# Attention's values products as split products over pairs of heads, and a state update over all 128 rows, in a two-layer hybrid decoder

## The chip, the core and the metric

The kernel runs on one core of a Trainium2 chip. The metric is the device time of one execution in microseconds. Five engines work side by side, each through its own instructions in order: TensorE (PE; its weight loads are shown apart as PEld), VectorE (DVE), ScalarE (ACT), POOL and SP, which issues all transfers. TensorE writes into PSUM, here eight banks of 128x512 float32.

## The reference

Two layers of a decoder over 512 prompt tokens and 64 sample tokens (8 sequences of 8). In each layer one widened projection feeds two branches, retention and sparse attention; both are gated, projected and merged. The parts that the change touches are these, cut to their core:

```python
# sparse attention, per query block of 128 (q: 8 heads of 64, 2 key/value heads)
score = einsum('bths,bth->bts', relu(logits), iw * IDX_HEADS ** -0.5)
_, sel = top_k(where(causal, score, -inf), topk)
att = einsum('btkgd,btjkd->btkgj', qg, kg) * ATT_HEAD_DIM ** -0.5
p = softmax(where(valid, att, -inf))
o = einsum('btkgj,btjkd->btkgd', p, vg)          # the values product
u_a = einsum('bte,ed->btd', o * silu(az), w_o_att)
# retention, state of a sequence after its chunk (4 heads, 128x128 each)
S = S * decay_s + einsum('bchd,bche->bhde', kc * decay_k, vc)
```

All is float32; the kernel's result has to agree with it closely, so operands of fast products are split into a leading part and a remainder.

## The kernel before

Activations lie as 128 rows by tokens: `xh` and `xl` are the leading part and the remainder of the normalised input (float32r, a faster form of float32 on TensorE). Weights come in units of 128x1024, land in `wst` and are split into `whi` (ScalarE) and `wlo` (VectorE) by `convert`. A projection (`proj_a`) runs three products per block, `xh*whi`, `xl*whi` and `xh*wlo`, 288 columns each, into a `pm` bank. These are the "main" or "ordinary" products; 611 of them stand between 160 and 324 us.

Work is written as generators (streams): projections in the order of `PLAN`, and beside them streams for the indexer's top-k, for prompt attention (`attend`), for the samples' attention (`attend_s`) and for retention (`ret_p`, `ret_s`). `Streams.go` picks one instruction at a time: the one whose engine and inputs a model says are free first, ties by priority. It keeps a clock per engine, durations from `_duration`, and hops between engines from `HOP` plus a margin. The instruction is emitted there, so every row of the profile has this one line, L293. What the table says thus sets the order on each engine, and that order is then fixed; the engines meet on the chip only through semaphores.

Attention for query block j (0 to 3), head by head (`head`, three in flight): two score products into the bank `tq`, a softmax on VectorE and ScalarE in a tile of `t2k`, j+1 transposes into the bank `ta`, a ScalarE copy to another `t2k`, and j+1 values products into the bank `oT`. A values product has V as its weights (128 rows by 64 columns, in a part of a tile that the profile names `xl`), so it uses half of the array's columns, the tile form 128\*64; both operands are plain float32, and each such product is two records in the trace. A bank `oT` gathers all eight heads of a block, then one VectorE product of 128x512 gates it into `silz`.

The samples' state update (`ret_s`, per head and group g) multiplies the masked values `vt` (512 columns; leading parts on 64 rows, remainders on the other 64) by `kh`, the leading part of the keys on both halves, and then by `kl`, the keys' remainder, on 64 rows only, the tile form 64\*128. Both go into one `tr` bank. `kh`, `kl`, `vt` are tiles `iqs` in the profile.

POOL does the powers of the norms, 128x2 to 128x5, and nothing else of weight. At the end of a layer's attention, `layer` waits until all side streams are emitted, and then splits the gated branches `silz` into `oh` and `ol` for the output weights (the merge).

Of the kernel before, what the change touches and what calls it, by code (L numbers as in the profile page):

```python
# [105 lines left out]
class Op:  # L106
    __slots__ = ("eng", "fn", "a", "k", "name", "outs", "ins", "dur")

    def __init__(self, eng, fn, name, a, k):
# [4 lines left out]
        self.outs = [_box(x) for x in (out, acc) if x is not None]  # L114
        self.ins = [_box(x) for x in aps if x is not out and x is not acc]
# [26 lines left out]
def _duration(eng, name, out, aps, a, k):  # L142
    n = max(_free(x) for x in aps)
    psum = any(x.space == PSUM for x in aps[1:])
    if eng == "PE":
# [3 lines left out]
        if lhs.dtype == FT:  # L149
            if _free(lhs) <= 32:  # L150
                return 0.030 + n * 0.4e-3
            return 4 * max(n, 64) / 2.4e3 * (0.55 if _free(lhs) <= 64 else 1.0)
        return max(n, 64) / 2.4e3 + 0.003
# [10 lines left out]
    if eng == "POOL":  # L164
        return 0.3 + 0.165 * n
# [29 lines left out]
class Streams:  # L195
    """Emits the instructions of many sequential streams in the order in which a model of the engines could
    start them, so that each engine's program order follows what is ready."""
# [5 lines left out]
    def __init__(self):  # L203
# [5 lines left out]
        self.count = 0  # L209

# [66 lines left out]
    def go(self):  # L277
        clock = self.clock
        while True:
# [13 lines left out]
            op.fn(*op.a, **op.k)  # L293
            end = start + op.dur
# [10 lines left out]
def tile_hybrid_decoder(ctx: ExitStack, tc: tile.TileContext, A, O):  # L305
# [30 lines left out]
    def r3(ap, a):  # L336
        return ap.rearrange("p (a b) -> p a b", a=a)
# [54 lines left out]
    # ---- weights: one ordered sequence of units, each split into two float32r parts as it lands  # L392
# [164 lines left out]
    def layer(l, xh, xl, kxb):  # L557
# [32 lines left out]
        av = r3(raw[1][:, ro + 1152:ro + 1792], 5)  # L590
# [20 lines left out]
        T2 = slots(at, "t2k", [128, 512], FT, NSLOT["t2"])  # L611
# [66 lines left out]
        def kx(j, ps):  # L678
# [6 lines left out]
            kk = r3(kkt[:n], 3)  # L685
            yield S.activation(kkt[:n], src[:, 0:192], AF.Copy, scale=r)
            yield S.activation(av[:n, j], src[:, 192:320], AF.Copy, scale=r)
# [30 lines left out]
            yield SP.dma_start(O["v"][l, rows], av[:n, j])  # L718
# [179 lines left out]
        def head(j, u, g, kv, oT, done):  # L898
            L = max(256, (j + 1) * 128)
            bias = con("cb") if j == 0 else scs[j]  # L900
            q = qst[j, u][:, (g % 2) * 2 + kv]
            P = yield Get(T2)
# [5 lines left out]
            PT = yield Get(T2)  # L908
            pT = yield Get(BANK["ta"])
            W_ = (j + 1) * 128  # L910
            for k in range(j + 1):
                yield PE.transpose(pT[:, k * 128:(k + 1) * 128], P[:, k * 128:(k + 1) * 128], ident)
            K.put(T2, P)
            yield S.activation(PT[:, :W_], pT[:, :W_], AF.Copy)
            K.put(BANK["ta"], pT)
            for k in range(j + 1):
# [634 lines left out]
```

## Time and profile before

| | us |
|---|---|
| timed runs (3) | 1131.04, 1131.97, 1132.43; median 1131.97 |
| span of the profiled execution | 1130.3 |
| TensorE busy, matmul / weight loads | 1116.5 / 1058.9 |
| VectorE busy | 725.6 |
| ScalarE busy | 512.5 |
| POOL busy | 45.7 |

The profiled execution is told by its span, from the first to the last instruction; of its time outside the span the profile says nothing, so the span is set beside the median of the timed runs, 1.7 us longer. Busy times are unions of records, which may overlap: a matmul's record holds its way through the array, so a stream of products looks busy throughout, and the starts of its records tell how fast it runs. The granted clock of TensorE is 1.00 in every stretch (2.4 GHz).

### The profile page before, as it was taken

Reading aid. Unit: us, or ns where it says so; the run is one execution under the profiler, and the core shown is the slowest. Engines: PE = TensorE matmul, PEld = TensorE weight load, DVE = VectorE, ACT = ScalarE, POOL = GpSimd, SP = SyncE. Lnnn points to the kernel's source line nnn. Section 1 sums busy time; section 2 is a strip of 40 time slices with the busy share of each in tenths; the row PEclk is TensorE's granted clock in tenths of the full one; section 3 lists DMA queues with packets and bytes.
Section 4 is the critical chain, followed back from the end, with each engine's and each line's share of the span. In section 5 each row is a group of like instructions: output and inputs, shape, how many; then the busy total and the mean of one; then the engine's idle time right before and its main releaser. Section 6 shows DMA issues by size and latency. Waiting matters only on the chain.

```text
span 1130.3 us, 21562 instructions
## 1 busy us (share of the span) xinstructions
PE 1116.5 (99%) x8586; PEld 1058.9 (94%) x8586; DVE 725.6 (64%) x1883; ACT 512.5 (45%) x1084; POOL 45.7 (4%) x52
## 2 busy tenths in 40 slices
PE   8999999999999999999999999999999999999998
PEld 7899988888899999999999999888889999999998
DVE  6799988876464444543658999888654553544343
ACT  6643566647443232324546336656563422222331
POOL 0100200000000000000010012000000000000000
PEclk9999999999999999999999999999999999999999
DMA  6442221322122222523336112222212222234231
GB/s 196 139 133 76 76 75 52 102 78 78 59 75 75 93 76 92 172 92 109 100 118 181 59 57 94 74 79 80 73 60 78 75 78 91 75 130 144 93 113 48
DMA packets 43895, 105.92 MB, mean 94 GB/s; under 512 B 6418, under 2 KB 18578, under 8 KB 43794
## 3 DMA queue, kind: packets, MB, share of 16 engines
q1 hardware_dynamic: 43794, 104.55, 27.4%
q8 instruction: 67, 1.10, 0.4%
q14 instruction: 34, 0.28, 0.1%
HBM read 93.61 MB, written 10.91 MB: 92 GB/s over the span
## 4 chain that ended last, share of the span: by engine, by line
PE 91%; DVE 4%; DMA 2%; ACT 2%; issue 1%; SPq 0%; POOL 0%; DVEq 0%; ACTq 0%; POOLq 0%
PE pm L293 72%; PE oT L293 5%; PE tq L293 4%; PE acc L293 3%; PE tr L293 3%; PE ta L293 3%; DVE wlo L293 1%; DMA wst<-in_wb 1%; ACT whi L293 1%; DVE misc L293 1%; DMA x<-in_xT 1%; DVE silz L293 0%; DMA wst<-in_wq 0%; DVE qs L293 0%; DVE ol L293 0%
## 5 line engine op out<-in xcount | busy, mean ns | idle before, releaser
L293 PE MATMUL pm<-xl,whi 128*128 128x288 f32 x1536 | 458.7, 299 | 0.0
L293 PE MATMUL pm<-xh,wlo 128*128 128x288 f32 x1536 | 458.4, 298 | 0.0
L293 PE MATMUL pm<-xh,whi 128*128 128x288 f32 x1536 | 458.0, 298 | 0.4 <-DVE misc L293 0.4
L293 PEld LDWEIGHTS pm<-xl,whi 128*128 128x128 f32 x1536 | 290.1, 189 | 3.2 <-issue 2.4
L293 PEld LDWEIGHTS pm<-xh,whi 128*128 128x128 f32 x1536 | 290.2, 189 | 2.9 <-issue 1.6
L293 PEld LDWEIGHTS pm<-xh,wlo 128*128 128x128 f32 x1536 | 289.9, 189 | 1.8 <-issue 1.4
L293 ACT ACTIVATE whi<-wst 128x1024 fp32r<-128x1024 f32 (+4 forms) x148 | 150.5, 1019 | 280.5 <-PE pm L293 207.7
L293 DVE TENSOR_TENSOR wlo<-wst,whi 128x1024 fp32r<-128x1024 f32 (+4 forms) x148 | 173.0, 1171 | 88.8 <-ACT whi L293 88.5
L293 PE MATMUL pm<-whi,xh 128*128 128x256 f32 (+2 forms) x416 | 117.2, 288 | 0.7 <-ACT xl L293 0.7
L293 PE MATMUL pm<-wlo,xh 128*128 128x256 f32 (+2 forms) x416 | 117.0, 289 | 0.0
L293 PE MATMUL pm<-whi,xl 128*128 128x256 f32 (+2 forms) x320 | 91.0, 284 | 0.0
L293 DVE TENSOR_TENSOR misc<-pm,R 128x288 f32<-128x288 f32 x64 | 29.2, 457 | 90.1 <-PE pm L293 88.7
L293 ACT ACTIVATE t2k<-t2k,sm 128x256 f32<-128x256 f32 (+3 forms) x136 | 75.6, 581 | 22.6 <-DVE sm L293 19.4
L293 PEld LDWEIGHTS pm<-whi,xh 128*128 128x128 f32 x416 | 78.7, 189 | 2.5 <-issue 1.2
L293 PEld LDWEIGHTS pm<-wlo,xh 128*128 128x128 f32 x416 | 78.7, 189 | 1.6 <-issue 1.1
L293 PE MATMUL pm<-oh,whi 128*128 128x288 f32 x240 | 71.0, 296 | 0.0
L293 PE MATMUL pm<-oh,wlo 128*128 128x288 f32 x240 | 70.9, 296 | 0.0
L293 PE MATMUL pm<-ol,whi 128*128 128x288 f32 x240 | 70.9, 295 | 0.0
L293 PEld LDWEIGHTS pm<-whi,xl 128*128 128x128 f32 x320 | 60.5, 189 | 0.1
L293 ACT ACTIVATE misc<-misc 128x288 f32<-128x288 f32 x64 | 27.9, 436 | 60.5 <-DVE misc L293 60.5
L293 DVE MAX8 sm<-xl 128x8 f32<-128x384 f32 (+2 forms) x96 | 52.3, 548 | 0.3
L293 DVE SCALAR_TENSOR_TENSOR misc<-misc,pm 128x288 f32<-128x288 f32 x60 | 26.8, 451 | 39.3 <-PE pm L293 39.3
(231 smaller groups left out, 1654.3 us busy)
## 6 DMA issues: line engine op xcount, KB each, us to landing
wst<-in_wa SPq DMA_DIRECT2D x96, 512.0 KB, 3.5
wst<-in_wb SPq DMA_DIRECT2D x16, 512.0 KB, 4.1
wst<-in_wo SPq DMA_DIRECT2D x16, 512.0 KB, 3.4
s<-in_ckv SPq DMA_DIRECT2D x32, 128.0 KB, 2.4
s<-in_s SPq DMA_DIRECT2D x8, 512.0 KB, 4.3
out_rss<-s SPq DMA_DIRECT2D x8, 512.0 KB, 2.6
x<-in_xT SPq DMA_DIRECT2D x8, 288.0 KB, 4.5
misc<-in_xT SPq DMA_DIRECT2D x8, 288.0 KB, 3.6
```

Source lines behind the costliest of these rows:

```text
L293: op.fn(*op.a, **op.k)
```

## The change

Values products go by pairs of heads (`pair`, two pairs in flight). V is split once per block of 128 tokens into `vhl`: for each key/value head 128 columns, 64 leading and 64 remainder. The two heads' softmaxes (`score`) run as streams of their own; their transposes go in chunks of up to two blocks into one `ta` bank, 256 or 512 columns. ScalarE copies the chunk to `pth` (float32r) and VectorE takes the remainder `ptl`; there is one tile of each. Each block then takes two products with `vhl` as weights, 128 rows by 128 columns, and 256 columns of `pth` or `ptl`. The `oT` bank holds two pairs, the two halves of its rows being the sums with V's leading part and with its remainder; `collect` adds the halves (a ScalarE copy and a VectorE addition per key/value head, 64x256) and POOL multiplies by the gate. The state's `kl` is written to all 128 rows, so its second product also runs over 128 rows. The table of durations gets new numbers for TensorE, a small price for a change of tile form, and a price per column for POOL's products that are no power.

```diff
--- before.py
+++ after.py
@@ -112,6 +112,7 @@
         out = k.get("out", a[0] if a else None)
         acc = k.get("accum_out")
         self.outs = [_box(x) for x in (out, acc) if x is not None]
+        self.form = (_val(a[1].partition_size) > 64, min(2, _free(a[1]) - 1 >> 5)) if eng == "PE" else None
...
@@ -149,8 +150,8 @@
         if lhs.dtype == FT:
             if _free(lhs) <= 32:
                 return 0.030 + n * 0.4e-3
-            return 4 * max(n, 64) / 2.4e3 * (0.55 if _free(lhs) <= 64 else 1.0)
-        return max(n, 64) / 2.4e3 + 0.003
+            return 2 * max(0.11, n / 1.2e3 + 0.005)
+        return max(0.108, (n + 32) / 2.4e3)
...
     if eng == "POOL":
-        return 0.3 + 0.165 * n
+        return 0.3 + (0.165 if k.get("op", a[-1]) == OP.pow else 0.0022) * n
...
@@ -291,6 +293,9 @@
             op = st[3]
             start = best[0][0]
             op.fn(*op.a, **op.k)
+            if op.form != self.form and op.eng == "PE":
+                start += 0.09
+                self.form = op.form
             end = start + op.dur
...
+            if j < 4:
+                for i, (h, o) in enumerate(((0, 64), (192, 128))):
+                    vh = vhl[:, j, h:h + 64]
+                    yield S.activation(vh, v[:, i * 64:(i + 1) * 64], AF.Copy)
+                    yield V.tensor_tensor(vhl[:, j, o:o + 64], v[:, i * 64:(i + 1) * 64], vh.bitcast(FT), OP.subtract)
             K.put(T2, kt2)
@@ -895,53 +910,87 @@
             yield S.activation(P, P, AF.Copy, scale=s)
             K.put(SM, sm)
 
-        def head(j, u, g, kv, oT, done):
+        def score(j, q, kv, P):
             L = max(256, (j + 1) * 128)
             bias = con("cb") if j == 0 else scs[j]
-            q = qst[j, u][:, (g % 2) * 2 + kv]
-            P = yield Get(T2)
             b = yield Get(BANK["tq"])
             ps = b[:, :L]
             yield PE.matmul(ps, q, kdh[:, 1 + kv, :L], start=True, stop=False)
             yield PE.matmul(ps, q, kdl[:, 1 + kv, :L], start=False, stop=True)
             yield from softmax(ps, bias, P[:, :L], b)
-            PT = yield Get(T2)
-            pT = yield Get(BANK["ta"])
-            W_ = (j + 1) * 128
-            for k in range(j + 1):
-                yield PE.transpose(pT[:, k * 128:(k + 1) * 128], P[:, k * 128:(k + 1) * 128], ident)
-            K.put(T2, P)
-            yield S.activation(PT[:, :W_], pT[:, :W_], AF.Copy)
-            K.put(BANK["ta"], pT)
-            for k in range(j + 1):
-                yield PE.matmul(oT[kv * 64:(kv + 1) * 64, g * 128:(g + 1) * 128], av[:, k, kv * 64:(kv + 1) * 64],
-                                PT[:, k * 128:(k + 1) * 128], start=k == 0, stop=k == j)
-            K.put(T2, PT)
-            K.put(HD, None)
+
+        def pair(j, u, kv, oT, first, done):
+            Ps, evs = [], []
+            for i in range(2):
+                P = yield Get(T2)
+                ev = Event()
+                K.spawn(then(score(j, qst[j, u][:, i * 2 + kv], kv, P), ev), PRIO["attend"])
+                Ps.append(P)
+                evs.append(ev)
+            o = oT[:, kv * 256:(kv + 1) * 256]
+            for k0 in range(0, j + 1, 2):
+                ks = range(k0, min(k0 + 2, j + 1))
+                w = len(ks) * 256
+                pT = yield Get(BANK["ta"])
+                for i in range(2):
+                    yield evs[i]
+                    for k in ks:
+                        yield PE.transpose(pT[:, (k - k0) * 256 + i * 128:(k - k0) * 256 + (i + 1) * 128],
+                                           Ps[i][:, k * 128:(k + 1) * 128], ident)
+                if ks[-1] == j:
+                    for P in Ps:
+                        K.put(T2, P)
+                    K.put(HD, None)
+                hi = yield Get(PTH)
+                lo = yield Get(PTL)
+                yield S.activation(hi[:, :w], pT[:, :w], AF.Copy)
+                yield V.tensor_tensor(lo[:, :w], pT[:, :w], hi[:, :w].bitcast(FT), OP.subtract)
+                K.put(BANK["ta"], pT)
+                for k in ks:
+                    for x in (hi, lo):
+                        yield PE.matmul(o, vhl[:, k, kv * 128:(kv + 1) * 128], x[:, (k - k0) * 256:(k - k0 + 1) * 256],
+                                        start=not first, stop=k == j and x is lo, skip_group_check=True)
+                        first.append(None)
+                K.put(PTH, hi)
+                K.put(PTL, lo)
             K.set(done)
 
-        HD = Slots([None] * HEADS_IN_FLIGHT)
+        HD = Slots([None] * PAIRS_IN_FLIGHT)
+
+        def collect(j, u, oT, done):
+            yield done
+            t = yield Get(T2)
+            o = t[:, :256]
+            for kv in range(2):
+                mine, other = slice(kv * 64, kv * 64 + 64), slice(64 - kv * 64, 128 - kv * 64)
+                c = slice(kv * 256, (kv + 1) * 256)
+                yield S.activation(o[mine], oT[other, c], AF.Copy)
+                yield V.tensor_tensor(o[mine], oT[mine, c], o[mine], OP.add)
+            K.put(BANK["oT"], oT)
+            yield e_az
+            z = silz[1][:, 2 * u:2 * u + 2, j * 128:(j + 1) * 128]
+            yield G.tensor_tensor(z, r3(o, 2), z, OP.mult)
+            K.put(T2, t)
...
         def attend():
             yield e_k
+            last = []
             for j in range(4):
                 if j:
                     yield e_sc[j]
-                oT = yield Get(BANK["oT"])
-                done = Event(8)
                 for u in range(2):
                     yield e_q[j, u]
-                    for g in (2 * u, 2 * u + 1):
-                        for kv in range(2):
-                            yield Get(HD)
-                            K.spawn(head(j, u, g, kv, oT, done), PRIO["attend"])
-                yield done
-                for u in range(2):
+                    oT = yield Get(BANK["oT"])
+                    done, first = Event(2), []
+                    for kv in range(2):
+                        yield Get(HD)
+                        K.spawn(pair(j, u, kv, oT, first, done), PRIO["attend"])
+                    last.append(Event())
+                    K.spawn(then(collect(j, u, oT, done), last[-1]), PRIO["attend"])
+                    yield done
                     K.put(QS, qst[j, u])
-                yield e_az
-                z = silz[1][:, :, j * 128:(j + 1) * 128]
-                yield V.tensor_tensor(z, r3(oT, 4), z, OP.mult)
-                K.put(BANK["oT"], oT)
+            for ev in last:
+                yield ev
...
@@ -1146,12 +1195,14 @@
             ins, vs = t["ins"], vr[:NS, 4, hc]
             g8 = math.exp(8 * lg[h])
             ks = yield Get(IQS)
-            kh, kl, vh = ks[:, 0], ks[:NS, 1], ks[:, 2]
+            kh, kl, vh = ks[:, 0], ks[:, 1], ks[:, 2]
             yield V.memset(ins[:NS, NS:96], 0.0)
             yield V.tensor_tensor(ins[:NS, :NS], b[:NS, :NS], con("blk", NS), OP.mult)
             yield S.activation(kh[:NS], b[:NS, 128:256], AF.Copy, scale=g8)
             yield S.activation(kh[NS:], b[:NS, 128:256], AF.Copy, scale=g8)
-            yield V.scalar_tensor_tensor(kl, b[:NS, 128:256], g8, kh[:NS].bitcast(FT), op0=OP.mult, op1=OP.subtract)
+            for rows in (slice(0, NS), slice(NS, 128)):
+                yield V.scalar_tensor_tensor(kl[rows], b[:NS, 128:256], g8, kh[:NS].bitcast(FT), op0=OP.mult,
+                                             op1=OP.subtract)
             K.put(BANK["tr"], b)
...
@@ -1182,7 +1233,7 @@
                                       bc(con("mk")[:, g * 4:g * 4 + 4, None], [128, 4, 128]), OP.mult)
                 pn = yield Get(BANK["tr"])
                 yield PE.matmul(pn, kh, flat(vt), start=True, stop=False)
-                yield PE.matmul(pn, kl, flat(vt)[:NS], start=False, stop=True)
+                yield PE.matmul(pn, kl, flat(vt), start=False, stop=True)
...
 PLAN = _plan("kx iq rv0 rv1 az0 az1 az2 az3 aq0 aq1 rt0 rt1 rt2 rt3")
-HEADS_IN_FLIGHT = 3
+PAIRS_IN_FLIGHT = 2
 PRIO = dict(convert=0, load=1, tables=6, indexer=7, indexer_s=3, attend=3, attend_s=5, ret_p=6, ret_s=4)
-NSLOT = dict(s4=3, qs=5, t2=5, hi=3, lo=3)
+NSLOT = dict(s4=3, qs=4, t2=5, pt=1, hi=3, lo=3)
```

How this moves instructions is shown at three places of layer 1, near the end of attention. TensorE, before: heads of block 3 (`oT` are values products, `ta` transposes, `tq` scores, `pm` main products).

```order
L293 MATMUL pm_68<-xh,wlo_93 128x288
L293 MATMUL pm_68<-xh,whi_90 128x288
L293 MATMUL oT_73<-t2k_386,xl 64x128 x4
L293 MATMUL ta_72<-cst,t2k_385 128x128 x4
L293 MATMUL tq_71<-kdh,qs_378 128x512
L293 MATMUL tq_71<-kdl,qs_378 128x512
L293 MATMUL pm_68<-xl,whi_90 128x288
```

And now, the last two pairs of block 3 but one chunk:

```order
L295 MATMUL oT_73<-pth_392,vhl 128x256
L295 MATMUL pm_68<-xh,whi_90 128x288
L295 MATMUL pm_68<-xl,whi_90 128x288
L295 MATMUL pm_68<-xh,wlo_93 128x288
L295 MATMUL pm_68<-xh,whi_90 128x288
L295 MATMUL pm_68<-xl,whi_90 128x288
L295 MATMUL oT_73<-ptl_393,vhl 128x256
L295 MATMUL oT_73<-pth_392,vhl 128x256
L295 MATMUL oT_73<-ptl_393,vhl 128x256
L295 MATMUL ta_72<-cst,t2k_395 128x128 x2
L295 MATMUL ta_72<-cst,t2k_397 128x128 x2
L295 MATMUL pm_68<-xh,wlo_93 128x288
```

Four products of a head in a row have become products in a chain of one, then three; the product of `ptl` stands behind five main products, and the next chunk's transposes follow it directly.

VectorE, before, at the gating of the last `oT` bank of layer 1 (`xh`, `iqs`: retention of the samples; `misc`: a gate's projection):

```order
L293 MEMSET xh 64x32
L293 TENSOR_TENSOR xh<-tr_74,cst 64x64
L293 SCALAR_TENSOR_TENSOR iqs_375<-tr_74,iqs_375 64x128
L293 TENSOR_TENSOR iqs_375<-xh,iqs_375 64x128
L293 TENSOR_TENSOR silz_358<-oT_73,silz_358 128x4x128
L293 TENSOR_TENSOR misc<-pm_69,R 128x288
```

And now, from the third last chunk's remainder to the last additions:

```order
L295 TENSOR_TENSOR ptl_393<-ta_72,pth_392 128x512
L295 TENSOR_TENSOR gs_406<-gs_406,cst 128x4
L295 SCALAR_TENSOR_TENSOR gs_406<-gs_406 128x4
L295 TENSOR_TENSOR misc<-pm_69,R 128x288
L295 TENSOR_TENSOR wlo_92<-wst_87,whi_89 128x1024
L295 TENSOR_TENSOR ptl_393<-ta_72,pth_392 128x512
L295 TENSOR_TENSOR silz_367<-tr_74,silz_367 128x512
L295 TENSOR_TENSOR misc<-pm_70,R 128x288
L295 TENSOR_TENSOR ptl_393<-ta_72,pth_392 128x512 x2
L295 TENSOR_TENSOR misc<-pm_68,R 128x288
L295 TENSOR_TENSOR wlo_93<-wst_88,whi_90 128x1024
L295 TENSOR_TENSOR t2k_396<-oT_73,t2k_396 64x256 x2
```

The one product on `oT` is gone; remainders `ptl` stand between weight conversions `wlo` and evacuations, and two additions on `oT` follow.

POOL, before, the last powers of layer 1's retention:

```order
L293 TENSOR_TENSOR gs_394<-rsm_96,mh 128x2
L293 TENSOR_TENSOR gs_395<-rsm_97,mh 128x4
L293 TENSOR_TENSOR gs_394<-rsm_98,mh 128x2
L293 TENSOR_TENSOR gs_395<-rsm_96,mh 128x4
L293 TENSOR_TENSOR gs_394<-rsm_97,mh 128x2
L293 TENSOR_TENSOR gs_395<-rsm_98,mh 128x4
```

And now, to the end of layer 1:

```order
L295 TENSOR_TENSOR silz_368<-t2k_396,silz_368 128x2x128
L295 TENSOR_TENSOR gs_405<-rsm_97,mh 128x2
L295 TENSOR_TENSOR silz_368<-t2k_396,silz_368 128x2x128
L295 TENSOR_TENSOR gs_406<-rsm_98,mh 128x4
L295 TENSOR_TENSOR silz_368<-t2k_396,silz_368 128x2x128
```

The gating products `silz` stand between the powers, in one queue; the last stands behind the last power.

## Rows read from the trace of the kernel before

**Rows 1.** The page: busy us by engine, and the chain of waits by engine
```profile
PE 1116.5 (99%) x8586; PEld 1058.9 (94%) x8586; DVE 725.6 (64%) x1883; ACT 512.5 (45%) x1084; POOL 45.7 (4%) x52
...
PE 91%; DVE 4%; DMA 2%; ACT 2%; issue 1%; SPq 0%; POOL 0%; DVEq 0%; ACTq 0%; POOLq 0%
```

**Rows 2.** Busy us (instructions) by stretch: PE, PEld, DVE, ACT, POOL; clock; DMA
```profile
0.00:57.00 57.00, 49.79 (x358) 47.81 (x359) 39.83 (x125) 37.77 (x86) 5.46 (x10) 1.00 0.53 168
57.00:113.00 56.00, 56.00 (x435) 53.44 (x435) 53.10 (x155) 21.37 (x44) 2.38 (x2) 1.00 0.31 103
160.00:324.00 164.00, 163.65 (x1323) 143.16 (x1323) 114.19 (x358) 93.90 (x231) 6.81 (x8) 1.00 0.21 73
334.00:580.00 246.00, 246.00 (x1848) 245.99 (x1847) 116.96 (x164) 84.56 (x137) 0.00 (x0) 1.00 0.30 102
718.00:882.00 164.00, 163.60 (x1325) 142.95 (x1324) 113.53 (x355) 94.05 (x231) 6.82 (x8) 1.00 0.21 73
```

**Rows 3.** Waits of TensorE, 160 to 324 us: total, times, longest
```profile
PE ta L293 <- ACT t2k L293: 0.2, 1, 0.2
```

**Rows 4.** Order in time on TensorE, one head's values products: start, us
```profile
275.88 0.29 PE L293 MATMUL pm<-xl,whi 128*128 128x288 f32 x1
276.10 1.09 PE L293 MATMUL oT<-t2k,xl 128*64 128x128 f32 x8
277.12 0.40 PE L293 MATMUL pm<-xh,wlo 128*128 128x288 f32 x1
277.35 0.29 PE L293 MATMUL pm<-xh,whi 128*128 128x288 f32 x1
```

**Rows 5.** Before and behind a group of two values records, layers 1 and 2
```profile
138.51 0.29 PE L293 MATMUL pm<-xl,whi 128*128 128x288 f32 x1
...
139.33 0.29 PE L293 MATMUL pm<-xh,whi 128*128 128x288 f32 x1
...
696.25 0.29 PE L293 MATMUL pm<-xl,whi 128*128 128x288 f32 x1
...
697.08 0.29 PE L293 MATMUL pm<-xh,whi 128*128 128x288 f32 x1
```

**Rows 6.** TensorE instructions on tile oT: min/median/max ns, first and last start
```profile
L293 PE MATMUL oT<-t2k,xl x320: 272/273/324, 126.6 to 854.3; 128*64 128x128 f32 x160
```

**Rows 7.** Order in time on TensorE, one pair of state products (x2)
```profile
260.31 0.83 PE L293 MATMUL tr<-iqs,iqs 128*128 128x512 f32 x2
...
261.31 0.29 PE L293 MATMUL pm<-xl,whi 128*128 128x288 f32 x1
```

**Rows 8.** Order in time on TensorE, two full products of 512 columns
```profile
278.21 0.40 PE L293 MATMUL tq<-kdh,qs 128*128 128x512 f32 x1
278.45 0.39 PE L293 MATMUL tq<-kdl,qs 128*128 128x512 f32 x1
```

**Rows 9.** Order in time on TensorE, full products of 256 columns
```profile
600.08 0.28 PE L293 MATMUL pm<-wlo,xh 128*128 128x256 f32 x1
...
600.67 0.28 PE L293 MATMUL pm<-whi,xl 128*128 128x256 f32 x1
```

**Rows 10.** VectorE groups by form, 150 to 330 us: busy us, mean ns, idle before
```profile
L293 DVE TENSOR_TENSOR wlo<-wst,whi 128x1024 fp32r<-128x1024 f32 x15 | 18.3, 1219 | 1.7 <-ACT whi L293 1.6
...
L293 DVE TENSOR_TENSOR silz<-oT,silz 128x512 f32<-128x512 f32 x4 | 2.7, 687 | 0.3 <-PE oT L293 0.3
...
L293 DVE TENSOR_TENSOR qs<-ta,qs 64x256 fp32r<-64x256 f32 x6 | 2.5, 422 | 1.2 <-ACT qs L293 1.0
...
L293 DVE SCALAR_TENSOR_TENSOR iqs<-tr,iqs 64x128 fp32r<-64x128 f32 x4 | 1.1, 279 | 0.7 <-ACT iqs L293 0.6
```

**Rows 11.** POOL: two single powers in order of time
```profile
124.47 1.01 POOL L293 TENSOR_TENSOR sm<-rsm,mh 128x4 f32<-128x4 f32 x1 [1.54 <-DVE rsm L293]
...
255.31 0.70 POOL L293 TENSOR_TENSOR gs<-rsm,mh 128x2 f32<-128x2 f32 x1 [17.03 <-DVE rsm L293]
```

**Rows 12.** Waits ahead of weight loads on oT, 160 to 324 us: us, times
```profile
  ACT t2k L293: 0.9, 5
```

More of the change, by code (lines that the diff above doesn't have):

```diff
@@ L106 @@
 class Op:
-    __slots__ = ("eng", "fn", "a", "k", "name", "outs", "ins", "dur")
+    __slots__ = ("eng", "fn", "a", "k", "name", "outs", "ins", "dur", "form")
     def __init__(self, eng, fn, name, a, k):
@@ L209, in __init__ @@
         self.count = 0
+        self.form = None
     def spawn(self, gen, prio):
@@ L589, in layer @@
         ro = 2 * (2 * T + 32)
-        av = r3(raw[1][:, ro + 1152:ro + 1792], 5)
+        avs = raw[1][:, ro + 1152:ro + 1280]
+        vhl = at.tile([128, 4, 256], FR, name="vhl")
         iqss = raw[1][:, ro + 1792:ro + 2048].rearrange("p (b h t) -> p b h t", b=8, h=4)
@@ L610, in layer @@
         QS = slots(at, "qs", [128, 4, 128], FR, NSLOT["qs"])
-        T2 = slots(at, "t2k", [128, 512], FT, NSLOT["t2"])
+        PTH = slots(at, "pth", [128, 512], FR, NSLOT["pt"])
+        PTL = slots(at, "ptl", [128, 512], FR, NSLOT["pt"])
+        T2 = slots(at, "t2k", [128, 512], FT, NSLOT["t2"] - 1)
+        T2.free.append(raw[1][:, ro + 1280:ro + 1792])
         S4 = slots(at, "s4", [128, 8, 128], FT, NSLOT["s4"])
@@ L685, in kx @@
             kk = r3(kkt[:n], 3)
+            v = kt2[:n, 192:320] if j < 4 else avs[:n]
             yield S.activation(kkt[:n], src[:, 0:192], AF.Copy, scale=r)
-            yield S.activation(av[:n, j], src[:, 192:320], AF.Copy, scale=r)
+            yield S.activation(v, src[:, 192:320], AF.Copy, scale=r)
             pulled(j, ps, z)
@@ L717, in kx @@
             yield SP.dma_start(O["k"][l, rows], flat(kv))
-            yield SP.dma_start(O["v"][l, rows], av[:n, j])
+            yield SP.dma_start(O["v"][l, rows], v)
+            if j < 4:
[3 more added lines that the diff above has]
+                    yield V.tensor_tensor(vhl[:, j, o:o + 64], v[:, i * 64:(i + 1) * 64], vh.bitcast(FT), OP.subtract)
             K.put(T2, kt2)
@@ L985, in attend_s @@
                     o = oS[:, kv * 64:(kv + 1) * 64]
-                    yield PE.matmul(o, PT[:NS, 256:384], av[:NS, 4, hb], start=True, stop=True)
+                    yield PE.matmul(o, PT[:NS, 256:384], avs[:NS, hb], start=True, stop=True)
                     for b4 in range(4):
```

## Prediction

> **What bounds the kernel now.** I read the page's first lines, then the chain of waits, then busy time by stretch, then the order in time of single matmuls. TensorE is busy 99% of the span and holds 91% of the chain that ended last [rows 1]. A busy matmul row says little by itself, so the stretches are the test [rows 2]. The change works in 160 to 324 us (attention and retention of layer 1) and in its twin 718 to 882 us. There the granted clock is 1.00 (the 2.4 GHz level), TensorE idles 0.35 us of 164, VectorE is busy 114.2 us (70%) and ScalarE 93.9 us (57%). The only wait of TensorE on another engine that the list of waits holds there is 0.2 us [rows 3]. So what leaves TensorE's queue there should leave the time, as long as the others keep up.
>
> **What one values product costs TensorE now.** The starts in time tell more than the durations, which overlap. Ordinary 288-column products start 0.133 us apart (in a stretch of these alone 1848 take 246.0 us, [rows 2]). In [rows 4] the last product before a head's eight values records starts at 275.88 and the second one after them at 277.35: 1.47 us, less two ordinary products (0.27) is 1.21 us for the group (four products, two records each). In [rows 5] the same reckoning for a group of two records gives 139.33 - 138.51 - 0.27 = 0.56 us. Hence (1.21 - 0.56)/6 = 0.108 us a record, and 0.56 - 0.22 = 0.34 us that belong to entering and leaving the tile form 128\*64, 0.17 us each way. The gaps are seen in the starts: 0.22 us ahead of the group, then 0.23 us between the two ordinary products behind it.
>
> **The sum on TensorE, both layers.** Removed:
> - 320 values records [rows 6] at 0.108: 34.6 us.
> - Changes of tile form. Counted along TensorE's order, neighbours of different tile form fall from 294 to 151. At 0.17 us, 143 of them are 24.3 us. (64 heads and 16 state updates would give 160; 17 are lost because other small tiles now stand alone.)
> - The second state product of each pair, 64 rows by 512 columns, 16 times (two layers, four heads, two groups). In [rows 7] the pair starts at 260.31 and the second ordinary product behind it at 261.31; less 0.13 and less 0.23 for the first, full product (512 columns start 0.23 to 0.24 us apart, [rows 8]) this leaves 0.64, of which 0.34 are form changes already counted. 16 x 0.30 = 4.8 us.
>
> Added: 160 products of 256 columns in the full form. Such products take five spacings in 0.59 us [rows 9], 0.118 each: 18.9 us. And 16 full products of 512 columns at 0.23: 3.7 us. Scores, transposes and projections are the same in number. Net: 63.7 - 22.6 = 41 us less.
>
> **The other engines, per layer.** VectorE gets 24 remainders, 16 of 128x512 at 0.69 us and 8 of 256 columns at 0.42; 16 additions of 64x256 at 0.42; 4 second remainders of the state (64x128) at 0.28; 8 of V, 64 columns, at no more than that; and loses four 128x512 products at 0.69 [rows 10]: 11.0 + 3.4 + 6.7 + 1.1 + 2.2 - 2.8 = 22 us, 2 of them ahead of the stretch. In the stretch that is 114 + 20 = 134 us of 164 - 20 = 144 us, 93%. What makes me think it is carried: from 57 to 113 us VectorE is busy 53.1 of 56 us, 95%, and TensorE idles nothing [rows 2]. ScalarE copies the same columns of P in fewer pieces and gains 16 copies of 64x256 and 8 of 64 columns; at VectorE's 0.42 and 0.28 that is 9 us, to 103 of 144. If VectorE's cover went, each remainder that is late would hold TensorE, since its product stands in order with everything behind it.
>
> **POOL** gets 16 products of 128x256 with two SBUF inputs; the trace has no such operation. Bounds: VectorE's 0.42 us for that size from below, and from above the slope of POOL's power, 0.70 us at two columns and 1.01 at four [rows 11], 0.155 us a column, 40 us each. I take 1 us, near the lower row, since a power is not a multiplication. At 1 us it is hidden: the layer's last one stands 29 main products (3.9 us) ahead of the split that opens the merge. The Trainium skill speaks against the place: GPSIMD Engine Reference, Engine selection, gives elementwise work to VectorE and calls GpSimd about twice as slow with two inputs; its 4497 ns for 2048 columns would be, as an estimate, 0.56 us here. No row shows it, and the sum would not move.
>
> **New waits.** A chunk's two forms are now fetched one after the other, ScalarE's, then VectorE's, and there is one buffer of each: 48 chunks, 96 hand-overs. Low bound nothing, as TensorE waits now. High bound: the weight loads of the values products waited 0.9 us in 5 cases [rows 12], 0.18 us each; on all 96 that is 17 us. Since the order puts about five main products between a chunk's two forms, I take a quarter, 4 us. The new durations also reorder the start, where TensorE idles 7.2 us of the first 57 [rows 2]: plus or minus 3 us, taken as zero. Behind a late remainder stand the transposes of the next chunk, then main products, then evacuation.
>
> The profile's span is 1130.3 us; the median of the timed runs, 1131.97, lies 1.7 us above it, taken as fixed. 1130.3 - 41 + 4 + 1.7 = **1095 us**, own range 1087 to 1104.
>
> **Rivals.**
> - *The remainders become the bound* (still faster). VectorE is in order, and a weight conversion is 1.22 us [rows 10]. With one of them in front of half the 48 chunks, TensorE stands 24 x 1.22 = 29 us: 1120 us; with a third of that, 1101. For it: 93% busy, one buffer, and a single bank each for transposes and output. Against it: the 95% stretch from 57 us on, in which VectorE's weight conversions ran beside a full TensorE too.
> - *The gaps around small tiles are waits, not the price of the form.* Weight loads are busy 143 of 164 us in the stretch, against 246 of 246 where only full products run [rows 2]. If the 24 us were waits for softmax results, they would stay: 1131.97 - (34.6 + 4.8 - 22.6) = 1115 us. Against it: a group of two costs the same 0.56 us in layer 2 (697.08 - 696.25 - 0.27, [rows 5]) as in layer 1, and the list of waits has nothing of that size [rows 3]. The Trainium skill, Perfetto Trace Analysis, Identifying the Most-Contended Engine, would have me judge TensorE by that weight-load share and see headroom here. The Trainium skill, TensorEngine Tiling (Array Packing), Key Properties, says a change of tiling mode drains the engine; by that rule the gaps go with the forms, and the equal 0.34 us agree.
> - *POOL's products decide* (slower). At the upper bound, eight of 40 us take 320 us in a stretch of 144: 176 us more per layer, about 1091 + 352 = 1443 us. From 18 us a product on POOL outlasts the stretch, from about 20 it eats the gain of 20 us a layer. For it: only the slope of the power, the one operation of POOL that the trace times at several widths. Against it: the slope belongs to another operation, and VectorE takes 0.42 us for a product of this size.
> - *It doesn't do what it says*: the new products run at twice the spacing. 160 x 0.118 more, 1114 us. Against it: the projections' products of this size and type keep the 0.118 [rows 9].
>
> **How the numbers follow.** Forecast 0.76, remainders 0.13, gaps that stay 0.05, POOL 0.03, double spacing 0.03. The range takes in most of the remainder case on the high side and a gain at the start on the low side: 1086 to 1111. A difference of 0.2% (2.3 us) can be told from none. Slower: POOL's 0.03 and 0.01 for remainders far worse than worked out. Same: 0.02, from the tails. Faster: 0.94.
>
> **What would show it.** In the new profile TensorE stays over 98% busy, and the stretches of attention shrink by about 20 us in each layer, the rest staying as it is. The list by form shows no 128\*64 values records and no 64\*128 state products. The 256-column values products start 0.12 us apart, with ordinary gaps around them. VectorE rises to some 768 us in total and stays under 95% in the stretch. POOL's products show about 1 us. Wrong would be: TensorE waiting on `ptl` or `pth` for over 10 us in total, idle time at the merge (last values product to the first product of the output weights), or POOL products in tens of us.

## The result and the profile after

The changed kernel takes 1152.2 us (median of 4 runs, 1149.4 to 1153.7) against 1131.7 us: ratio 1.018, 95% interval 1.016 to 1.019. It is 20 us slower; the forecast was 1095 us. The rows that follow are of its profiled execution, the quickest of the four (span 1147.4 us).

The page of the changed kernel, busy time by engine and the chain by engine (answering [rows 1]):

```profile
PE 1099.3 (96%) x8426; PEld 1054.0 (92%) x8426; DVE 762.7 (66%) x1979; ACT 525.9 (46%) x1116; POOL 57.9 (5%) x68
...
PE 68%; DVE 23%; ACT 4%; issue 2%; DMA 2%; SPq 0%; POOL 0%; DVEq 0%; ACTq 0%; POOLq 0%
```

TensorE is now idle for 48 us of the span, and VectorE holds 23% of the chain instead of 4%. Where that is, the stretches tell; first one row of the kernel before that [rows 2] left out, then the changed kernel. The columns are those of [rows 2], and the number ahead of the DMA share is the granted clock.

```profile
113.00:160.00 47.00, 46.64 (x349) 42.83 (x348) 43.39 (x145) 28.32 (x69) 8.56 (x8) 1.00 0.23 80
```

```profile
57.00:113.00 56.00, 54.99 (x425) 52.08 (x424) 55.54 (x162) 21.67 (x43) 0.80 (x1) 1.00 0.29 92
113.00:160.00 47.00, 36.59 (x255) 34.14 (x254) 43.86 (x149) 20.51 (x47) 9.36 (x10) 0.89 0.15 46
160.00:324.00 164.00, 158.26 (x1290) 142.85 (x1289) 123.38 (x377) 103.25 (x253) 12.71 (x15) 0.99 0.24 79
...
718.00:882.00 164.00, 157.29 (x1273) 141.47 (x1273) 124.64 (x382) 100.77 (x248) 12.06 (x15) 0.99 0.22 76
```

The largest hole is not in attention but ahead of it: from 113 to 160 us, the end of the top-k stage, TensorE issues 255 products instead of 349. Its waits there, from 126 to 170 us (waited for: total us, times, longest):

```profile
PE ta L295 <- DVE qs L295: 4.3, 3, 2.6
PE pm L295 <- DVE misc L295: 1.9, 2, 1.3
PE pm L295 <- ACT t2k L295: 1.4, 1, 1.4
```

TensorE waits for the preparation of q (`qs`, `misc`), never long for `ptl` or `pth`. The chain of waits from 126 us on (start, us, what) shows what VectorE did meanwhile:

```profile
126.41 0.46 DVE sm L295
126.88 0.66 DVE xl L295
...
128.80 1.11 DVE sm L295 x3
129.91 1.19 DVE xl L295 x2
131.10 0.60 DVE sm L295
131.70 0.34 DVE ptl L295
132.08 0.44 PE ta L295 x2
```

`xl` and `sm` are top-k steps (the scores lie in `xl`). Counted up to the start of the 875th projection product (those into the `pm` banks, in order), the kernel before had started 28 such steps over 128 rows and the changed one 43. The 16 of them with 256 columns are the same in both; the others are these, before up to that point (0 to 153 us), then after (0 to 168 us):

```profile
L293 DVE MAX8 sm<-xl 128x8 f32<-128x384 f32 x10 | 5.5, 554 | 0.0
...
L293 DVE MAX8 sm<-xl 128x8 f32<-128x512 f32 x2 | 1.4, 680 | 0.0
```

```profile
L295 DVE MAX8 sm<-xl 128x8 f32<-128x384 f32 x16 | 8.8, 549 | 0.1
...
L295 DVE MAX8 sm<-xl 128x8 f32<-128x512 f32 x11 | 7.5, 683 | 0.0
```

These 15 steps go with the hole, but steps alone do not make it. By the same count two of the runs below, e1 and g1, have 38 and 37 steps, and between the 700th and the 775th projection product they stand about 1 us each, where the changed kernel stands 13.

What the prediction said of TensorE's own work came true. Its order in time, three values products between projection products (answering [rows 4]):

```profile
303.51 0.29 PE L295 MATMUL pm<-xl,whi 128*128 128x288 f32 x1
303.64 0.28 PE L295 MATMUL oT<-ptl,vhl 128*128 128x256 f32 x1
303.76 0.28 PE L295 MATMUL oT<-pth,vhl 128*128 128x256 f32 x1
303.88 0.28 PE L295 MATMUL oT<-ptl,vhl 128*128 128x256 f32 x1
304.00 0.29 PE L295 MATMUL pm<-xh,wlo 128*128 128x288 f32 x1
```

They are 0.12 us apart, and there is no gap ahead or behind. So I split each span of TensorE in three, by the prices of the prediction: every product at its undisturbed spacing (kinds that the prediction does not price, at the usual spacing of their own kind), 0.17 us for each change of tile form, and the rest, called *standing* below (waits and the time lost at a lower clock).

| kernel | products | changes of form | standing |
|---|---|---|---|
| before | 1061.7 | 50.0 | 5.9 |
| changed | 1044.7 | 25.7 | 64.4 |

Other prices for the rare kinds would shift all these standings alike, by up to some 6 us; their differences move by about 0.5 us at most. Products and forms fell by 41.3 us, the 41 of the forecast. Standing rose by 58.5 us, where 4 were forecast. Of the changed kernel's standing, 22 us lie between the 500th and the 1000th projection product (100 to 199 us) and 20 us between the 3900th and the 4300th (672 to 753 us), the same stages of the two layers. The kernel before stands 1 to 2 us in each. Another 18 us lie in the stretches of attention and retention (199 to 333 us and 753 to 860 us), where the kernel before stands 2 us in all. TensorE's waits listed there come to 3.1 and 4.4 us, only 0.2 us of them for `ptl`; the rest of these 18 us is not traced to a cause.

### The profile page after: what moved, and what is told of

It is laid out like the page before. It is cut to its first block, busy times and chain, and to the rows that moved or that the text cites. A ratio compares the mean times of both kernels' runs of the same rounds, so it can differ in the third digit from the quotient of the medians.

```text
span 1147.4 us, 21421 instructions
## 1 busy us (share of the span) xinstructions
PE 1099.3 (96%) x8426; PEld 1054.0 (92%) x8426; DVE 762.7 (66%) x1979; ACT 525.9 (46%) x1116; POOL 57.9 (5%) x68
## 3 DMA queue, kind: packets, MB, share of 16 engines
q8 instruction: 66, 1.08, 0.4%
## 4 chain that ended last, share of the span: by engine, by line
PE 68%; DVE 23%; ACT 4%; issue 2%; DMA 2%; SPq 0%; POOL 0%; DVEq 0%; ACTq 0%; POOLq 0%
PE pm L295 56%; DVE xl L295 6%; DVE sm L295 5%; DVE wlo L295 3%; PE acc L295 3%; PE tq L295 3%; PE oT L295 3%; DVE misc L295 2%; PE tr L295 2%; PE ta L295 2%; DVE t2k L295 1%; DVE silz L295 1%; DVE qs L295 1%; ACT t2k L295 1%; ACT tb L295 1%
## 5 line engine op out<-in xcount | busy, mean ns | idle before, releaser
L295 PE MATMUL pm<-whi,xh 128*128 128x256 f32 (+2 forms) x416 | 119.5, 293 | 5.5 <-DVE misc L295 2.7
L295 ACT ACTIVATE t2k<-t2k,sm 128x256 f32<-128x256 f32 (+3 forms) x111 | 62.5, 578 | 33.2 <-DVE sm L295 30.6
L295 DVE MAX8 sm<-xl 128x8 f32<-128x512 f32 (+2 forms) x96 | 52.4, 549 | 0.5
L295 DVE MATCH_REPLACE8 xl<-sm,xl 128x256 f32<-128x256 f32 (+2 forms) x96 | 51.7, 540 | 0.1
```

## The experiments

Each run changes the kernel before or the changed one; the interval is that of the ratio to the kernel before. Standing is read from the profiled execution, which need not be the median one: that of l1 is its quickest (1112.6 us), that of n1 its slowest (1136.1 us).

| run | base | us | ratio (95%) | standing |
|---|---|---|---|---|
| e1 | before, new durations | 1156.4 | 1.020 to 1.024 | 29.9 |
| e2 | changed, old durations | 1161.6 | 1.024 to 1.028 | 78.8 |
| e3 | changed, old main number | 1151.7 | 1.016 to 1.019 | 68.2 |
| e4 | before, state on 128 rows | 1132.3 | 1.000 to 1.001 | 10.5 |
| g1 | changed, bank later | 1135.3 | 1.002 to 1.005 | 50.0 |
| g2 | g1, old durations | 1157.2 | 1.022 to 1.026 | 73.1 |
| f1 | changed, five q buffers | 1155.0 | 1.020 to 1.023 | 69.1 |
| h1 | before, bank earlier | 1207.2 | 1.066 to 1.069 | 80.6 |
| i1 | g1, no barrier | 1132.5 | 1.000 to 1.001 | 48.0 |
| i2 | g2, no barrier | 1120.2 | 0.988 to 0.991 | 36.1 |
| i3 | i1, old main number | 1130.9 | 0.998 to 1.000 | 43.0 |
| k1 | i1, others x1.09, x1.15 | 1142.8 | 1.008 to 1.011 | 57.7 |
| k2 | e1, others x1.09, x1.15 | 1141.7 | 1.008 to 1.011 | 14.3 |
| k4 | i1, others x1.05, x1.08 | 1121.2 | 0.989 to 0.993 | 34.3 |
| l1 | i2, form price | 1115.9 | 0.985 to 0.988 | 28.0 |
| n1 | l1, new main number | 1132.5 | 1.000 to 1.002 | 52.4 |
| n2 | before, new main number | 1140.6 | 1.007 to 1.010 | 12.7 |
| n3 | before, new fp32 number | 1134.1 | 1.001 to 1.003 | 6.7 |

**Durations or structure?** e1 and e2 swap the tables; e3 undoes one number. The lines are shown as changes to the changed kernel, and the comments say in which run they stand.

```diff
-        return max(0.108, (n + 32) / 2.4e3)    # main: e2, e3
+        return max(n, 64) / 2.4e3 + 0.003
...
-            return 2 * max(0.11, n / 1.2e3 + 0.005)    # fp32: e2
+            return 4 * max(n, 64) / 2.4e3 * (0.55 if _free(lhs) <= 64 else 1.0)
...
-                start += 0.09    # price of a form: e2
+                start += 0.0
```

e1 (the reverse of this on the kernel before). 

> The kernel before with the changed kernel's durations and its form price in the scheduler, nothing else. Two theories of the 58 us that TensorE loses to stalls in the changed kernel (64 us against 6 by its order of work). A, the durations: TensorE's ordinary product goes from 0.123 to 0.133 in the table, so the scheduler puts more of VectorE's top-k work ahead of the preparation of q and leaves VectorE no slack; TensorE then waits in the top-k stages (57 to 160 and 640 to 740 us): this kernel should lose there as the changed one does, 15 us in the first layer and 15 in the second, about 1160 us. B, the structure (fewer buffers, split values, remainders): the durations alone do nothing, 1132 us give or take 3.

e2. 

> The changed kernel with the durations before for TensorE (ordinary product 0.123 of 288 columns, fp32 products as before, no price for a change of form); POOL's product keeps its new, small number. A, the durations: the stalls of the top-k stages go, TensorE's work stays 41 us lower: 1100 us (1095 to 1115, the upper end because the last values products now stand right ahead of the output projection and may hold it). B, the structure: the stalls stay, 1152 us give or take 5.

e3. 

> The changed kernel with one number undone, that of TensorE's ordinary product (0.133 back to 0.123); the fp32 number and the price of 0.09 for a change of form stay. If the ordinary product's number is what fills VectorE's queue (A): as with all old numbers, about 1100 us. If it is the price of the form or the fp32 number: as the changed kernel, about 1150 us. B: 1152 us.

e1 bore out theory A: the durations alone cost 24 us. About 13 us of its added standing lie in the top-k stages and 8 in the stretches of attention. e2 refuted A, which had it at 1115 us at most, and went beyond B's 1157: with the old durations the changed structure is slower still. So both harm, and not additively. First e1 in the stretch with the hole, then e2 there and at the merge of layer 1 (columns as above):

```profile
113.00:160.00 47.00, 43.67 (x320) 38.80 (x319) 45.07 (x156) 26.22 (x65) 9.35 (x9) 1.00 0.18 57
```

```profile
113.00:160.00 47.00, 37.98 (x256) 35.78 (x255) 41.73 (x142) 22.73 (x53) 7.75 (x8) 0.85 0.14 46
...
304.00:345.00 41.00, 33.04 (x187) 29.27 (x187) 23.75 (x55) 21.58 (x45) 2.44 (x3) 0.75 0.12 41
```

The structure makes the hole at 113 to 160 us whatever the table (e1, without it, has a small one); the old table adds another at the merge, where attention now ends too late. e3 left the first as it was and half of the second.

**The state update alone.** e4 has the diff's two hunks on `kl` and nothing else. 

> The kernel before with only the state update's second product on 128 rows instead of 64 (16 products, the second remainder written twice). By the prediction's terms: 16 x 0.30 us of records and 16 x 0.34 us of form changes go, less 3.7 us for 16 full products of 512 columns: 6.5 us less, about 1125 us. If the gaps around small tiles are waits, not the price of the form: 1131 us. The table is that of before, so the top-k stages should show no stall under either theory.

```profile
309.99 0.30 PE L293 MATMUL pm<-xh,whi 128*128 128x288 f32 x1
310.13 0.63 PE L293 MATMUL tr<-iqs,iqs 128*128 128x512 f32 x2
310.60 0.49 PE L293 MATMUL acc<-xh 128*128 128x128 f32 x3
```

The gaps went, as the form's price says (0.47 us for the pair, against 1.00 for the pair and one ordinary product in [rows 7]): products and forms fell by 5.1 us. But the time did not move, and standing rose by 4.6 us. My 6.5 us were wrong as a time, and 1132 us is what the rival theory gave (gaps that are waits); the rows decide against it. The order of instructions is another one, since changes of form fell by 24 and not by 32. That the new order makes TensorE stand is likely but not shown.

**The held bank.** In the changed kernel a pair of heads takes the one bank for transposes (`ta`), and only then waits for its two softmaxes. The q of the following blocks is transposed through the same bank. g1 and g2 turn that round, h1 does it to the kernel before, f1 tests the rival of too few q buffers.

```diff
-                pT = yield Get(BANK["ta"])
-                for i in range(2):
-                    yield evs[i]
+                for ev in evs:
+                    yield ev
+                pT = yield Get(BANK["ta"])
+                for i in range(2):
```

```diff
 # h1, in head()
+            pT = yield Get(BANK["ta"])
             b = yield Get(BANK["tq"])
...
-            pT = yield Get(BANK["ta"])
 # f1
-NSLOT = dict(s4=3, qs=4, t2=5, pt=1, hi=3, lo=3)
+NSLOT = dict(s4=3, qs=5, t2=5, pt=1, hi=3, lo=3)
```

g1. 

> The changed kernel with one thing moved: a pair of heads takes the bank for its transposes (there is one, and the q of the next blocks are transposed through it too) only when both its softmaxes are done, as the kernel before did for a head; the new durations stay. The changed kernel takes it first and keeps it while the softmaxes run, so q's preparation, and the products queued behind it, wait in the top-k stage (13 us between the 700th and the 775th projection product of layer 1, the like in layer 2). Theory C, the held bank: those 13 us a layer go, about 1152 - 26 = 1126 us, and what the new durations cost (24 us on the kernel before) is still in it. Theory S, four buffers for q instead of five: nothing changes, 1152 us give or take 4.

g2. 

> The bank taken after the softmaxes and TensorE's old durations, both. If C and the durations are the two causes and add up, what is left is TensorE's work, 41 us less than before, and the cost of the merge: with the old durations the last values products stand right ahead of the output projection (17 us of stall in each layer when the bank was held). Without that stall 1095 us, with half of it 1112, with all of it 1127 us. Theory S: 1160 us.

f1 (its fifth buffer costs a `t2k` buffer of 512 columns, which comes back only when k is prepared, in a space that other steps share; attention's values are then not the reference's, and f1 is read for its time alone). 

> The changed kernel with five buffers for q instead of four (the space comes from a buffer of 512 columns that is only free again once k is prepared); bank and durations as changed. Theory S: the top-k stages lose their stall, 1126 us. Theory C: the bank is still held, 1150 us give or take 5.

h1. 

> The reverse on the kernel before: a head takes the transposes' bank ahead of its scores and keeps it through its softmax; nothing else. Theory C: q's preparation stops in the top-k stage as in the changed kernel, 13 us a layer or more since heads now follow one another, and attention ends late: 1160 to 1200 us. If the held bank costs nothing (TensorE has other work to do meanwhile): 1132 us, give or take 5.

The same stretch in g1, in f1, and in h1:

```profile
113.00:160.00 47.00, 42.44 (x324) 39.92 (x323) 45.48 (x155) 25.90 (x61) 8.79 (x10) 1.00 0.17 58
```

```profile
113.00:160.00 47.00, 35.65 (x235) 33.56 (x235) 43.52 (x151) 20.75 (x50) 10.24 (x10) 0.85 0.13 46
```

```profile
113.00:160.00 47.00, 35.75 (x241) 32.51 (x240) 44.30 (x141) 19.46 (x44) 6.96 (x7) 0.85 0.13 46
```

The held bank is shown from both sides. Taking it later brings back 69 products and the full clock in the stretch, and 17 us of time (26 expected: the hole between the 700th and the 775th product went from 13.0 to 1.3 us, but other standing took some back). Taking it early opens the hole in the kernel before, and costs 76 us there, more than the 69 I gave at most. These 76 us are not the price of the hole: some 31 us of the added standing lie in the top-k stages and some 41 at the merges. TensorE's longest wait in h1 is the one ahead of a head's transposes, for that head's own softmax, since the three heads in flight now take the bank in turn:

```profile
PE ta L293 <- ACT t2k L293: 28.6, 23, 2.6
```

Theory S, too few buffers for q, is refuted by g1, which has four and no hole; f1 agrees, but it has one `t2k` buffer less at first, so that alone it would not settle it. g2 is nearest to the 1160 us of S, but for another reason: ahead of the merge it was 20 us quicker than before (the 1525th product starts at 304.0 us, against 324.0), then it stood 23 us at the merge, and 26 in layer 2.

**The barrier.** A group of four heads starts only when the one before has finished. i1, i2 and i3 let the next group's first pair do its scores and softmaxes meanwhile.

```diff
-                    oT = yield Get(BANK["oT"])
-                    done, first = Event(2), []
+                    box, got, done, first = [], Event(), Event(2), []
+                    K.spawn(bank(box, got), PRIO["attend"])
                     for kv in range(2):
+                        if kv:
+                            yield got
                         yield Get(HD)
...
-                    yield done
-                    K.put(QS, qst[j, u])
```

`bank` fetches the output bank and sets `got`; a pair waits for it behind its softmaxes, and `collect` gives the q buffer back.

i1. 

> The changed kernel with the bank taken after the softmaxes (1135 us with that alone), and the next group of four heads may run its first pair's scores and softmaxes while the group before still multiplies values; it takes the output bank only when its own softmaxes are done. New durations. Theory D: attention is a chain of groups that drain one by one, and its end is late. With the new durations the merge has no stall of its own (0.3 us), so D expects little here, 1125 to 1135 us. Theory V, VectorE's load: the top-k and conversion work that the new durations put ahead of TensorE stays, 1135 us give or take 4.

i2. 

> The same without barrier, with TensorE's old durations. With the barrier this took 1157 us, of which 23 and 26 us were stalls ahead of the output projection, while everything ahead of that point was 20 us a layer quicker than before. D: the stalls at the merge go, 1157 - 49 = 1108 us, 1100 at best. V: the end of attention is set by VectorE's work and not by the barrier, the stalls stay, 1145 us or more.

i3. 

> The same without barrier, with only the ordinary product's number old (0.123); the fp32 number and the price of a form change stay new, which makes TensorE slower in the scheduler inside attention alone. D: like the old durations or better, 1100 to 1108 us, since attention's end gets some more room ahead of the merge and the top-k stage keeps the old, looser order. If the price of the form is what costs (a stall spread over the top-k stage as with all new durations): 1130 us.

The merge of layer 1 with the old durations, with the barrier (g2) and without (i2):

```profile
304.00:345.00 41.00, 29.60 (x137) 23.29 (x137) 19.76 (x38) 18.52 (x34) 1.45 (x2) 0.67 0.04 13
```

```profile
304.00:345.00 41.00, 37.85 (x262) 36.26 (x261) 24.29 (x49) 15.68 (x30) 1.75 (x2) 0.92 0.23 77
```

In g2 VectorE and ScalarE are both idle half the time while TensorE stands: a chain of short steps, not a load. Without the barrier that is worth 37 us (49 expected; some 14 us of the merges' standing stay). V is refuted for the old durations. With the new ones the barrier is worth 3 us; 1132.5 us lies in the ranges of D and of V, so that i1 does not tell them apart. i3 missed D's 1100 to 1108 and came out at the 1130 us of its other case.

**What in the durations harms?** k1, k2, k4 make VectorE and ScalarE longer in the table; l1 is i2 with the form's price; n1 to n3 put single numbers in. The line shown is that of k1 and k2; k4 has 1.05 and 1.08.

```diff
-        self.dur = _duration(eng, name, out, aps, a, k)
+        self.dur = _duration(eng, name, out, aps, a, k) * {"DVE": 1.09, "ACT": 1.15}.get(eng, 1.0)
```

k1. 

> As without barrier and with the new durations (1132 us), but VectorE's durations in the table times 1.09 and ScalarE's times 1.15. In the kernel before the table says 665 us of VectorE where the trace is busy 726, and 444 of ScalarE where it is busy 512, and it was as much too short for TensorE's ordinary product (0.123 against 0.133): all three alike. Theory R, the ratio: the new durations mend TensorE alone, so the scheduler takes VectorE for quicker against TensorE than it is and fills its queue; with all three mended the order loosens again and the time is that of the old durations or less: 1110 to 1122 us. Theory P, the price of forms and the fp32 number by themselves are bad for the order: 1132 us give or take 4, as before.

k2. 

> The same test on the kernel before: new TensorE durations and form price (1156 us alone), with VectorE times 1.09 and ScalarE times 1.15. R: back to 1132 us give or take 5. P: 1150 us or more.

k4. 

> As the first, but by half: VectorE times 1.05, ScalarE times 1.08. R: between the two, 1115 to 1128 us. P: 1132 us give or take 4. A dose that does not stand between the two would say that the order's time is not a smooth function of the ratio and that a single order is partly chance.

l1. 

> As without barrier and with TensorE's old durations (1120 us), but with the price of 0.09 for a change of form. With the fp32 number new as well it was 1131 us. R: a small price that hits attention alone changes little, 1120 us give or take 4. P, the price costs: 1131 us; if it is the fp32 number, 1120 us.

n1. 

> Without barrier and with the bank taken after the softmaxes; the ordinary product's number new (0.133), the price of a form new, the fp32 number old. All three new took 1132.5 us, only the form price new 1116 us. If the ordinary product's number is what fills VectorE's queue early (theory M): 1128 to 1136 us. If the fp32 number does it (theory F): 1116 us give or take 4.

n2. 

> The kernel before with the ordinary product's new number (0.133) and nothing else of the table. The whole new table cost 24 us here. M: most of that, 1148 to 1158 us. F: 1132 us give or take 4.

n3. 

> The kernel before with the new fp32 number alone (0.22 for a product that the old table has at 0.06 to 0.12). M: 1132 us give or take 4. F: most of the 24 us, 1148 to 1158 us.

The form's price does no harm on the mended kernel (l1). On the kernel before, the main number costs 9 us and the fp32 number 2, all of the table 24 (n2, n3, e1); the form's price was not run alone there, so the other 13 us may be its own or come of the three together. On the mended kernel the main number costs 17 us and the fp32 number 15 (n1 and i3 against l1), both together 17 (i1).

What the numbers do to VectorE's queue can be counted: the top-k steps over 128 rows that it has started by the 700th projection product.

| run | before | e1 | n2 | n3 | k2 | i1 | n1 | i3 | l1 |
|---|---|---|---|---|---|---|---|---|---|
| steps | 24 | 31 | 30 | 24 | 25 | 31 | 32 | 25 | 25 |

The main number puts six or seven steps ahead, and longer numbers for the other engines take them back. So far R, the ratio between the engines, is shown. That the time follows the count is not: k2, with 25 steps, gave back 15 of the 24 us and missed its 1132; n2, with 30, missed the ranges of M and of F; i3, with 25, is no quicker than n1 with 32. On the mended kernel half the dose takes back 11 us (k4), within R's range, but the full dose costs 10 more (k1) and lies outside the ranges of both R and P; its standing of some 18 us at the merge of layer 2 is the other failure, attention too late. By k4's own sign a dose that does not stand between the two says that a single order is partly chance. How much is chance stays open.

l1 is the best version: 1115.9 us, 1.4% under the kernel before and 3.2% under the changed one. Its page:

```profile
PE 1081.6 (97%) x8426; PEld 1044.4 (94%) x8426; DVE 760.0 (68%) x1979; ACT 523.2 (47%) x1116; POOL 58.4 (5%) x68
...
PE 82%; DVE 11%; ACT 4%; issue 1%; DMA 1%; SPq 0%; POOL 0%; ACTq 0%; DVEq 0%; POOLq 0%
```

It has the split products, the state on 128 rows, the old numbers with the form's price, the late bank and no barrier. In its profiled execution (span 1110.5 us) it still stands 28 us against 6, so 22 of the 41 us that TensorE was relieved of are not earned. Some 15 of the 28 us lie in the stretches of attention and retention; why is open.

## Why the prediction was wrong

- *The sum on TensorE* held: 41.3 us against 41, and the form's price as well (the three values products above, e4's pair). The Trainium skill, TensorEngine Tiling (Array Packing), Key Properties, has a change of tiling mode drain the engine. The trace agrees so far as a change has a price that goes with the form: 0.87 us for the state pair before, 0.47 us in e4.
- *"New waits"*, sized at 4 us, is the step that failed. It counted the hand-overs of the two forms, on which TensorE hardly waits. It did not read what a pair holds while it waits: the bank for transposes (17 us on the changed kernel, g1), and the turn of the next group (3 us behind that, i1; 37 us with the old durations, i2). The rival of the remainders did name the single bank, but not that q's preparation goes through it. Both stand in the diff, in the order of `Get`, `yield evs[i]` and `yield done`.
- *The durations*, "plus or minus 3 us, taken as zero", are the second: 24 us on the kernel before (e1), 17 us on the mended kernel (i1 against l1). I looked for their effect only at the start; half of it fell in the top-k stages and a third in attention.
- *The rest.* Of the 57 us between forecast and result, g1, i1 and l1 in turn take back 17, 3 and 17. The other 21 us, from l1's 1115.9 to 1095, have no shown cause.
- *"It is carried"* generalized from [rows 2]: VectorE 95% busy from 57 to 113 us beside a full TensorE. That showed that VectorE's queue was short enough then, not that it could take more. In the changed kernel TensorE is idle for 1.0 us of that stretch, with VectorE 99% busy, and it stands 9 and 10 us from 199 to 333 us and from 753 to 860 us, with VectorE only 68 and 73% busy. So the share of time in which VectorE is busy did not tell whether TensorE is kept fed.
- *The rivals.* The remainders as the bound: TensorE's waits for `ptl` come to 0.2 us for its products and 0.9 us for their weight loads, so no. Gaps that stay and double spacing: no, see the rows. POOL: its products take 0.79 us (I took 1), and hide:

```profile
L295 POOL TENSOR_TENSOR silz<-t2k,silz 128x256 f32<-128x256 f32 x12 | 9.4, 787 | 106.2 <-DVE t2k L295 106.2
```

The Trainium skill, GPSIMD Engine Reference, Engine selection, has GpSimd about twice as slow as VectorE with two inputs. The trace agrees: VectorE's remainder of the same 128x256, with one operand in PSUM, takes 415 ns. A slower kernel was given 0.04, and for mechanisms that played no part.

## What to carry to other kernels

When a change regroups work, read for each stream what it holds when it waits; a single bank or buffer held across a wait stops everyone who needs it, and that is seen in the code before any profile. A table of durations that orders instructions sets how much one engine's queue is filled ahead of another's: mending one engine's numbers alone moved that here, and cost 24 us on the kernel before. Such an edit is a change of its own, to be run by itself. Count busy work and standing apart, since a sum of busy work that is right to 1% can miss the time by 57 us.

## What the runs showed of the hardware

The granted clock fell where TensorE stood. In the changed kernel, by stretch:

```profile
130.00:140.00 10.00, 6.08 (x47) 5.31 (x45) 9.13 (x26) 4.01 (x11) 2.14 (x3) 1.00 0.00 0
140.00:145.00 5.00, 3.23 (x14) 2.83 (x15) 4.80 (x18) 1.40 (x3) 1.57 (x2) 0.52 0.00 2
145.00:150.00 5.00, 2.50 (x12) 1.87 (x11) 4.63 (x8) 3.46 (x7) 0.00 (x0) 0.80 0.32 107
150.00:155.00 5.00, 4.65 (x23) 4.65 (x24) 4.58 (x21) 0.60 (x2) 2.41 (x2) 0.66 0.36 106
155.00:160.00 5.00, 4.99 (x39) 4.75 (x38) 3.85 (x15) 2.66 (x6) 0.00 (x0) 1.00 0.00 0
```

After 10 us in which TensorE was busy 6.1, the clock was mostly at its lower level (0.52), and it stayed mixed until 155 us. From 150 to 155 us TensorE was busy 4.65 us and issued 23 products, where the next 5 us took 39. So a stall costs again after it has ended, by these counts some 1.7 us in that slice alone (an estimate: 5 us less 23/39 of it, less the 0.35 us in which TensorE was idle).
